# The low halves of the HGRN and mLSTM weights, formed by VectorE alone

## The chip, the cores and the metric

One core of one Trainium2 chip. The metric is the device time of one execution in microseconds, taken as the median of several runs. The profile is that of one further execution.

## The reference, cut to what matters

One layer over 256 latent tokens with 256 context tokens ahead of them, width 1024, all in fp32. A combined projection `w_in` feeds two recurrent branches: HGRN2 with 8 heads, and an mLSTM with 4 heads. Their outputs are merged and go through a mixture of 32 experts.

```python
p_lat = jnp.split(h_lat @ w_in + b_in, SEG_OFFSETS[:-1], axis=-1)
p_ctx = jnp.split(h_ctx @ w_in + b_in, SEG_OFFSETS[:-1], axis=-1)
...
o_ctx, hs_f, hs_b = hgrn_core(p_ctx[0], p_ctx[1], p_ctx[2], p_ctx[3], lb, s0, s0)
o_lat, _, _ = hgrn_core(p_lat[0], p_lat[1], p_lat[2], p_lat[3], lb, hs_f, hs_b)
...
for e in range(N_EXPERTS):
    a = jax.nn.silu(tok @ w_gate[e]) * (tok @ w_up[e])
    out = out + combine[:, e:e + 1] * (a @ w_down[e])
```

## The kernel before, in words

**How a product with `w_in` is made.** The fp32 weights arrive in tiles `raw` of 128x2048 (1 MB). Each is split into a high half `whi`, which ScalarE rounds in two copies of 1024 columns, and a low half `wlo = raw - whi`. The activations are split in the same way (`hhi`, `hlo`), and a product is three series of matmuls on TensorE: high by high (L362, or L371 where the weights are the stationary operand), low activations by high weights (L363, L372), and high activations by low weights (L365, L374). A split's `wlo` is thus the last thing that its product needs.

**Who forms the low half.** `load_split_` (L223 to L236) gives columns 0 to 256 x (8 - kp) to VectorE and the rest to GpSimd. The constant `KH` is the kp of the HGRN branch, `MKP` that of the mLSTM heads, `GKP` that of the merge and of the output projection. With `KH, MKP, GKP = 2, 3, 2` VectorE has 1536 columns of an HGRN split and GpSimd 512; in an mLSTM split it is 1280 and 768.

**Stages.** About 22 us of start, then the adaLN modulation and first products up to 57 us. Then HGRN works in four pairs of heads (p = 0 to 3) up to about 306 us, five splits a pair, of which the first two of p = 0 are formed elsewhere: 18 splits of `load_split`. The four mLSTM heads follow, three splits each (12 splits), up to about 440 us. The merge of the branches has 20 splits (`GKP`). From 565 us on the experts' weights stream in, and the matmuls of the experts follow them.

**What sets the order.** The code is written for a scheduler that puts the instructions of all engines into in-order queues, by priorities (`PRIO`) and by its own estimates of durations. An engine works down its queue; an instruction that waits holds up all behind it. The work of the next pair or head is thus laced into that of the present one. Buffers bound the lacing: `raw` has 3 tiles and one more in a ring, `whi` and `wlo` 2 each, and PSUM has 3 banks `mm`, 2 `lv`, 2 `oo` and a single bank `tp` for transposes.

**Names that come up below.** An HGRN pair has gates on VectorE and GpSimd (`fl`, `fc` at L635, L637; `kl`, `kc` at L641, L642), transposes of `kd` through `tp` (L698), state matmuls (L704), and eight levels, each with small matmuls (L720, L744) and updates of `xa` and `kl` on VectorE (L759, L762). `xa` is first formed by GpSimd (L708). The gates of the mLSTM are prepared in between as small operations (`gz`, `r`, `rr`, L543 to L579). A column of the modulation is summed up on VectorE (`adac`, L315 and L317), transposed through the same bank `tp` (L324) and read out of it by a reduction on VectorE (L326). An mLSTM head convolves `q` and `k` on VectorE (`cz`, L864 and L866), transposes `k` through `tp` (L897), sums its state (L907), copies it out on VectorE (`cs`, L908) and reads it in L949.

Of the kernel before, what the change touches and what calls it, by code (L numbers as in the profile page):

```python
# [19 lines left out]
NQ = NE // 4  # L20
CAP = 32
RZ, RP, RA, RB, RC = 2, 2, 2, 5, 7
KH, MKP, GKP = 2, 3, 2
NWARM, NW0 = 2, (7, 2, 1)
MLG = 2
ADP = (1, 3)
# [1458 lines left out]
```

## Time and profile before

| what | value |
|---|---|
| median of 3 runs | 1005.48 us (1004.79 to 1009.0) |
| the profiled execution's own time | 1005.86 us |
| its span in the trace | 1003.8 us |
| TensorE matmuls, busy | 862.8 us |
| VectorE, busy | 477.0 us |
| ScalarE, busy | 277.9 us |
| GpSimd, busy | 191.2 us, 130 instructions |
| moved by DMA | 290.50 MB, 289 GB/s on the mean |

The shares are means over stages with different limits. From 57 to 565 us TensorE is nearly always busy while the DMA engines are at a third to nine tenths; from 565 us on the DMA engines are busy throughout and TensorE is not. The profiled execution lies 0.4 us above the median, and 2.1 us of its time lie outside the span.

### The profile page before, as it was taken

Reading aid. Unit: us, or ns where it says so; the run is one execution under the profiler, and the core shown is the slowest. Engines: PE = TensorE matmul, PEld = TensorE weight load, DVE = VectorE, ACT = ScalarE, POOL = GpSimd, SP = SyncE. Lnnn points to the kernel's source line nnn. Section 1 sums busy time; section 2 is a strip of 40 time slices with the busy share of each in tenths; the row PEclk is TensorE's granted clock in tenths of the full one; section 3 lists DMA queues with packets and bytes.
Section 4 is the critical chain, followed back from the end, with each engine's and each line's share of the span. In section 5 each row is a group of like instructions: output and inputs, shape, how many; then the busy total and the mean of one; then the engine's idle time right before and its main releaser. Section 6 shows DMA issues by size and latency. Waiting matters only on the chain.

```text
span 1003.8 us, 15963 instructions
## 1 busy us (share of the span) xinstructions
PE 862.8 (86%) x6687; PEld 591.7 (59%) x6687; DVE 477.0 (48%) x908; ACT 277.9 (28%) x430; POOL 191.2 (19%) x130
## 2 busy tenths in 40 slices
PE   7999999979998999999999999767686767777865
PEld 3588897968978898999999644213031220313312
DVE  3678779798667988874465422102020110202002
ACT  4564433643323553444443210000000000000101
POOL 0053441535503232124434000000000000000000
PEclk9999999989999999999999999879778776978978
DMA  9733345255243445248887999999999999999996
GB/s 372 287 130 133 126 137 193 98 191 187 96 164 114 165 147 167 83 159 321 300 332 277 373 423 426 426 425 423 428 424 427 425 424 388 419 426 424 426 424 265
DMA packets 45610, 290.50 MB, mean 289 GB/s; under 512 B 5216, under 2 KB 10336, under 8 KB 11104
## 3 DMA queue, kind: packets, MB, share of 16 engines
q1 hardware_dynamic: 45248, 288.94, 72.8%
q8 instruction: 53, 0.87, 0.3%
q10 hardware_dynamic: 288, 0.52, 0.1%
q14 instruction: 21, 0.17, 0.0%
HBM read 288.23 MB, written 1.21 MB: 288 GB/s over the span
## 4 chain that ended last, share of the span: by engine, by line
issue 45%; PE 41%; DVE 8%; ACT 3%; DMA 2%; POOL 1%; SPq 0%; POOLq 0%; DVEq 0%; ACTq 0%
PE mm L365 5%; PE mm L362 5%; PE mm L363 5%; PE mm L374 2%; PE mm L372 2%; PE mm L371 2%; PE mm L1102 2%; PE mm L1099 2%; PE mm L1100 2%; DMA raw<-in_win_dram 2%; PE mm L412 2%; DVE wlo L158 1%; PE mm L1240 1%; ACT whi L155 1%; PE oo L952 1%
## 5 line engine op out<-in xcount | busy, mean ns | idle before, releaser
L158 POOL TENSOR_TENSOR wlo<-raw,whi 128x512 fp32r<-128x512 f32 (+1 forms) x50 | 112.7, 2254 | 197.4 <-ACT whi L155 166.3
L155 ACT ACTIVATE whi<-raw 128x1024 fp32r<-128x1024 f32 x104 | 105.6, 1052 | 104.6 <-POOL wlo L158 26.3
L362 PE MATMUL mm<-hhi,whi 128*128 128x256 f32 (+1 forms) x448 | 132.2, 322 | 0.0
L363 PE MATMUL mm<-hlo,whi 128*128 128x256 f32 (+1 forms) x448 | 130.1, 317 | 0.0
L158 DVE TENSOR_TENSOR wlo<-raw,whi 128x1536 fp32r<-128x1536 f32 (+2 forms) x54 | 108.1, 2004 | 34.1 <-ACT whi L155 30.6
L158 DVE TENSOR_TENSOR a<-a,mm 128x512 f32<-128x512 f32 x8 | 5.5, 688 | 233.5 <-PE mm L1240 233.5
L362 PEld LDWEIGHTS mm<-hhi,whi 128*128 128x128 f32 x448 | 85.5, 191 | 4.8
L363 PEld LDWEIGHTS mm<-hlo,whi 128*128 128x128 f32 x448 | 85.5, 191 | 4.4
L1378 POOL TENSOR_TENSOR rsn<-rsn,con 128x2 f32<-128x2 f32 x1 | 0.7, 698 | 434.7 <-DVE rsn L158 434.7
L365 PE MATMUL mm<-hhi,wlo 128*128 128x256 f32 (+1 forms) x448 | 80.7, 319 | 0.9 <-POOL wlo L158 0.9
L365 PEld LDWEIGHTS mm<-hhi,wlo 128*128 128x128 f32 x448 | 65.8, 191 | 5.8 <-POOL wlo L158 1.1
L1214 DVE SCALAR_TENSOR_TENSOR x<-oo,mod,x 128x256 f32<-128x256 f32 x56 | 24.4, 480 | 88.3 <-PE oo L1273 88.3
L1240 PE MATMUL mm<-ub,xg 128*32 128x512 f32 x304 | 50.3, 734 | 17.3 <-DMA ub<-in_eu_dram 9.9
L371 PE MATMUL mm<-whi,hhi 128*128 128x256 f32 x256 | 63.1, 284 | 0.0
L372 PE MATMUL mm<-whi,hlo 128*128 128x256 f32 x256 | 62.9, 283 | 0.0
L371 PEld LDWEIGHTS mm<-whi,hhi 128*128 128x128 f32 x256 | 49.1, 192 | 0.2
L372 PEld LDWEIGHTS mm<-whi,hlo 128*128 128x128 f32 x256 | 49.1, 192 | 0.1
L155 ACT ACTIVATE aT<-tp 128x512 f32<-128x512 f32 x8 | 4.8, 597 | 148.1 <-PE tp L1252 148.1
L1273 PE MATMUL oo<-owT,y 128*128 128x256 f32 x112 | 35.3, 470 | 8.6 <-ACT y L155 8.6
L1240 PEld LDWEIGHTS mm<-ub,xg 128*32 128x32 f32 x304 | 8.3, 120 | 56.4 <-DMA ub<-in_eu_dram 24.8
L1264 PE MATMUL lv<-uc,aT 128*32 128x512 f32 x280 | 36.1, 604 | 5.6 <-DMA uc<-in_ed_dram 5.6
L1273 PEld LDWEIGHTS oo<-owT,y 128*128 128x128 f32 x112 | 24.6, 230 | 27.4 <-ACT y L155 21.0
(391 smaller groups left out, 1588.3 us busy)
## 6 DMA issues: line engine op xcount, KB each, us to landing
uc<-in_ed_dram SPq DMA_DIRECT2D x35, 1024.0 KB, 19.8
raw<-in_win_dram SPq DMA_DIRECT2D x32, 1024.0 KB, 5.0
raw<-in_wm_dram SPq DMA_DIRECT2D x20, 1024.0 KB, 5.0
ub<-in_eg_dram SPq DMA_DIRECT2D x20, 1024.0 KB, 19.4
ub<-in_eu_dram SPq DMA_DIRECT2D x18, 1024.0 KB, 19.5
raw<-in_wada_dram SPq DMA_DIRECT2D x16, 1024.0 KB, 4.9
uB<-in_eu_dram SPq DMA_DIRECT2D x14, 1024.0 KB, 19.6
uc<-in_eu_dram SPq DMA_DIRECT2D x14, 1024.0 KB, 19.7
```

The source lines that it names most:

```text
L155: return S.activation(o, i, f, **kw)
L158: return (e or V).tensor_tensor(o, a, b, op=op)
L362: T.matmul(o, a, hhi[:, k, c0:c0 + n], start=(k == 0), stop=False)
L363: T.matmul(o, a, hlo[:, k, c0:c0 + n], start=False, stop=False)
L365: last = T.matmul(o, lo[:, k, 128 * m:128 * m + 128], hhi[:, k, c0:c0 + n], start=False, stop=(k == 7))
L371: T.matmul(o, hhi[:, k, c0:c0 + 128], hi[:, k, :], start=(k == 0), stop=False)
L372: T.matmul(o, hlo[:, k, c0:c0 + 128], hi[:, k, :], start=False, stop=False)
L374: T.matmul(o, hhi[:, k, c0:c0 + 128], lo[:, k, :], start=False, stop=(k == 7))
L1214: V.scalar_tensor_tensor(o, r[:, n * a:n * a + n], mod[:, 0, 40 + c + a:41 + c + a], o, op0=ALU.mult, op1=ALU.add)
L1240: last = T.matmul(r[32 * i:32 * i + 32, :], xg[:, k, 32 * i:32 * i + 32], W[k][:, 512 * i:512 * i + 512], start=(k == 0), stop=(k == 7), t ...
L1264: T.matmul(r[32 * i:32 * i + 32, 0:n], aT[:, k, 32 * i:32 * i + 32], w[k][:, o:o + n], start=(k == 0), stop=(k == 3), tile_position=(0, 32 ...
L1273: last = T.matmul(r[:, 256 * a_:256 * a_ + 256], y[:, 128 * (c + a_):128 * (c + a_) + 128], owT, start=True, stop=True)
```

## The change

`KH` and `MKP` become 0. With kp = 0 the loop in `load_split_` gives VectorE one operation of 2048 columns, and GpSimd's slice is empty and is left out. So 18 operations of VectorE grow from 1536 to 2048 columns, 12 grow from 1280 to 2048, and 30 operations of GpSimd (18 of 512 columns, 12 of 768) are gone. The 20 splits of the merge stay as they are.

```diff
-KH, MKP, GKP = 2, 3, 2
+KH, MKP, GKP = 0, 0, 2
```

The scheduler makes other queues from it. The order of the TensorE queue differs between about 252 and 1460 of its 2584 rows, which is from the second HGRN pair to the third mLSTM head; the merge and the experts keep theirs. Three places matter below.

The first is TensorE's queue where the HGRN pair p = 2 hands over to p = 3. L365 is the end of a product of p = 2, L698 the transpose of `kd` of p = 2, the 512-wide L362 and L363 are the first product of p = 3, and L720 the levels of p = 2. Before:

```order
L365 MATMUL mm<-hhi,wlo 128x256 x7
L698 MATMUL tp<-con,kd 128x128 x4
L365 MATMUL mm<-hhi,wlo 128x256
L720 MATMUL lv<-q,t_2210 32x32
L720 MATMUL lv<-xa,yk 32x32 x16
L720 MATMUL lv<-q,t_2210 32x32 x15
L362 MATMUL mm<-hhi,whi 128x512
L704 MATMUL oo<-v,kt 128x128 x4
```

Now, from the row in which that L698 stands:

```order
L698 MATMUL tp<-con,kd 128x128 x4
L362 MATMUL mm<-hhi,whi 128x512
L363 MATMUL mm<-hlo,whi 128x512
L720 MATMUL lv<-xa,yk 32x32 x16
L704 MATMUL oo<-v,kt 128x128 x4
L698 MATMUL tp<-con,kd 128x128 x2
L744 MATMUL lv<-xa,kl 32x32 x16
L698 MATMUL tp<-con,kd 128x128 x2
L704 MATMUL oo<-v,kt 128x128 x4
L324 MATMUL tp<-con,adac 128x128 x4
L365 MATMUL mm<-hhi,wlo 128x512 x3
```

The L365 is now at row 724, with all 8, and L698 follows 37 rows later: ahead of it come 30 of the 512-wide matmuls of p = 3 and four groups of L720.

The second is VectorE's queue at the same place, up to the reduction L326 that reads the bank `tp` out. Before (the wide `wlo` stands 8 rows ahead of these):

```order
L158 TENSOR_TENSOR v<-mm,br 128x512
L315 TENSOR_SCALAR adac<-raw,sgc 128x512
L575 TENSOR_SCALAR gz<-gz 40x128
L317 SCALAR_TENSOR_TENSOR adac<-raw,sgc,adac 128x512
L543 SCALAR_TENSOR_TENSOR gz<-gz,con 40x255
L317 SCALAR_TENSOR_TENSOR adac<-raw,sgc,adac 128x512
L158 TENSOR_TENSOR gz<-gz 40x256
L317 SCALAR_TENSOR_TENSOR adac<-raw,sgc,adac 128x512
L579 TENSOR_SCALAR gz<-gz,mle 40x256
L317 SCALAR_TENSOR_TENSOR adac<-raw,sgc,adac 128x512
L326 TENSOR_REDUCE mod<-tp 128x4
L317 SCALAR_TENSOR_TENSOR adac<-raw,sgc,adac 128x512
```

Now (the `wlo` of 2048 columns stands 23 rows ahead of these, and the `adac` operations directly behind it):

```order
L158 TENSOR_TENSOR v<-mm,br 128x512
L738 COPY_PREDICATED adg<-lm,lv 128x128
L759 TENSOR_TENSOR xa<-xa,tot_2242 128x128x2x2
L762 TENSOR_TENSOR kl<-kl,tot_2290 128x32x2x8
L158 TENSOR_TENSOR gz<-gz 40x256
L738 COPY_PREDICATED adg<-lm,lv 128x128
L759 TENSOR_TENSOR xa<-xa,tot_2266 128x64x2x4
L579 TENSOR_SCALAR gz<-gz,mle 40x256
L762 TENSOR_TENSOR kl<-kl,tot_2314 128x16x2x16
L326 TENSOR_REDUCE mod<-tp 128x4
L738 COPY_PREDICATED adg<-lm,lv 128x128
L759 TENSOR_TENSOR xa<-xa,tot_2290 128x32x2x8
```

The reduction has moved from 18 to 32 rows behind its `wlo`: the whole `adac` series (seven L317) and three updates each of `xa` and `kl` are now in front of it.

The third is TensorE's queue at the first mLSTM head, where `k` is transposed (L897) and the state read (L949). The 512-wide product is head 1's, as the 256-wide one in `lv` is. Before:

```order
L362 MATMUL mm<-hhi,whi 128x512
L897 MATMUL tp<-con,k 128x128 x2
L912 MATMUL lv<-q,k 128x256 x2
L907 MATMUL oo<-v,wk 128x257 x4
L362 MATMUL lv<-hhi,whi 128x256
L363 MATMUL lv<-hlo,whi 128x256
L362 MATMUL lv<-hhi,whi 128x256
L363 MATMUL lv<-hlo,whi 128x256
L362 MATMUL lv<-hhi,whi 128x256
L949 MATMUL oo<-cs,qi 128x257
```

Now:

```order
L365 MATMUL mm<-hhi,wlo 128x512 x2
L897 MATMUL tp<-con,k 128x128 x2
L912 MATMUL lv<-q,k 128x256 x2
L362 MATMUL lv<-hhi,whi 128x256
L363 MATMUL lv<-hlo,whi 128x256
L907 MATMUL oo<-v,wk 128x257 x4
L362 MATMUL lv<-hhi,whi 128x256
```

Ten more rows of head 1's product stand in front of L897, and the first L949 has gone from 8 rows behind it to 20.

## Rows read from the trace of the kernel before

**Rows 1.** Windows by stage: us, engines' busy time (instructions), PEclk, DMA share, GB/s.

```profile
187.00:255.00 68.00, 60.81 (x603) 53.12 (x602) 60.57 (x104) 34.90 (x49) 30.91 (x16) 0.95 0.45 160
...
306.00:340.00 34.00, 30.41 (x210) 27.93 (x209) 30.14 (x66) 13.71 (x24) 7.90 (x7) 1.00 0.51 159
...
640.00:1003.80 363.80, 259.54 (x1614) 85.10 (x1612) 49.00 (x121) 22.45 (x46) 0.70 (x1) 0.80 0.98 411
```

**Rows 2.** TensorE's waits: total, times, longest; windows 57:125, 125:187, 187:255, 275:306, 306:340, 374:410.

```profile
PE lv L720 <- DVE xa L759: 1.0, 1, 1.0
...
PE lv L720 <- DVE xa L759: 1.3, 1, 1.3
...
PE tp L698 <- DVE mod L326: 6.0, 1, 6.0
PE mm L365 <- POOL wlo L158: 0.9, 1, 0.9
...
PE lv L720 <- DVE xa L759: 1.6, 2, 1.3
...
PE tp L897 <- DVE k L158: 2.1, 1, 2.1
PE oo L949 <- DVE cs L908: 1.4, 1, 1.4
...
PE oo L949 <- DVE cs L908: 1.3, 1, 1.3
```

**Rows 3.** Windows of seven and eight us at TensorE's longest wait; columns as in Rows 1.

```profile
210.00:217.00 7.00, 1.01 (x7) 0.83 (x6) 6.99 (x17) 2.85 (x6) 0.00 (x0) 0.71 0.48 153
217.00:225.00 8.00, 8.00 (x155) 6.33 (x154) 7.92 (x12) 5.12 (x8) 2.57 (x1) 0.82 1.00 364
```

**Rows 4.** Timeline, VectorE, then GpSimd, ahead of that wait's end.

```profile
201.50 1.72 DVE L158 TENSOR_TENSOR wlo<-raw,whi 128x1536 fp32r<-128x1536 f32 x1
203.15 4.08 DVE L158 TENSOR_TENSOR r<-gz 8x256 f32<-8x256 f32 x2
...
215.44 0.67 DVE L326 TENSOR_REDUCE mod<-tp 128x4 f32<-128x512 f32 x1
...
200.95 4.59 POOL L158 TENSOR_TENSOR xa<-fl,q 128x1024 f32<-128x1024 f32 x1 [7.56 <-DVE q L656]
...
207.90 1.29 POOL L158 TENSOR_TENSOR wlo<-raw,whi 128x512 fp32r<-128x512 f32 x1
```

**Rows 5.** Timeline, GpSimd, then VectorE, of one HGRN split.

```profile
173.18 2.87 POOL L158 TENSOR_TENSOR wlo<-raw,whi 128x512 fp32r<-128x512 f32 x1 [8.11 <-ACT t L155]
...
173.14 1.76 DVE L158 TENSOR_TENSOR wlo<-raw,whi 128x1536 fp32r<-128x1536 f32 x1 [0.69 <-ACT t L155]
174.82 1.38 DVE L635 TENSOR_SCALAR fl<-sg,oml,lbt 128x256 f32<-128x256 f32 x1
```

**Rows 6.** Timeline, VectorE: a split of 1024 columns, and one `fl` operation by itself.

```profile
37.46 1.22 DVE L158 TENSOR_TENSOR wlo<-raw,whi 128x1024 fp32r<-128x1024 f32 x1
...
162.22 0.41 DVE L635 TENSOR_SCALAR fl<-sg,oml,lbt 128x256 f32<-128x256 f32 x1 [0.42 <-ACT sg L155]
```

**Rows 7.** Groups by form: count | busy us, mean ns | idle before, releasers.

```profile
L158 POOL TENSOR_TENSOR wlo<-raw,whi 128x512 fp32r<-128x512 f32 x38 | 86.2, 2270 | 157.3 <-ACT whi L155 126.2 <-PE mm L365 11.6 <-issue 8.4
...
L158 DVE TENSOR_TENSOR wlo<-raw,whi 128x1536 fp32r<-128x1536 f32 x38 | 77.4, 2038 | 32.9 <-ACT whi L155 29.4 <-PE mm L365 2.7 <-ACT t L155 0.7
...
L317 DVE SCALAR_TENSOR_TENSOR adac<-raw,sgc,adac 128x512 f32<-128x512 f32 x49 | 40.4, 824 | 0.5
...
L759 DVE TENSOR_TENSOR xa<-xa,tot 128x512 f32<-128x512 f32 x28 | 19.3, 691 | 3.9 <-PE lv L744 1.9 <-PE lv L755 1.3 <-PE lv L720 0.4
```

**Rows 8.** Timeline, TensorE: two neighbouring matmuls of a 512-wide product.

```profile
220.58 0.39 PE L362 MATMUL mm<-hhi,whi 128*128 128x512 f32 x1
220.81 0.40 PE L363 MATMUL mm<-hlo,whi 128*128 128x512 f32 x1
```

**Rows 9.** Timeline, VectorE, at the last HGRN pair and the first mLSTM head.

```profile
280.29 2.58 DVE L759 TENSOR_TENSOR xa<-xa,fl 128x512 f32<-128x512 f32 x1 [0.59 <-PE lv L720]
...
311.89 1.98 DVE L864 TENSOR_SCALAR cz<-qin,pk 128x256 f32<-128x256 f32 x1
...
326.96 3.13 DVE L158 TENSOR_TENSOR wlo<-raw,whi 128x1280 fp32r<-128x1280 f32 x1
```

## The prediction

> **What bounds the kernel now.** I read the windows by stage first, then TensorE's waits in the stages that matter, then the timeline around each wait. From 640 us to the end the DMA engines are at 0.98 of their time and move 411 GB/s while TensorE works 259.5 of 363.8 us: the experts' weights are the bound there, and the change doesn't touch them [rows 1]. Before the merge it is TensorE: 60.8 of 68 us from 187 to 255, 30.4 of 34 from 306 to 340. VectorE is close behind, 60.6 and 30.1 us of the same stretches. So in the stages that the change touches, time can be won only in TensorE's gaps, and few gaps hold nearly all of it: 6.0 us and 0.9 in the stretch from 187 to 255, 1.6 at the last HGRN pair, 2.1 + 1.4 at the first mLSTM head, 1.3 at the third, and 1.0 and 1.3 in the two stretches from 57 to 187 [rows 2]. That is 15.6 us. All but the 0.9, which waits for GpSimd, end with an operation of VectorE, and that one may be late for its own work, for GpSimd's, or for its place in the queue. A gap closed ahead of the experts should reach the end nearly whole, since the experts' buffers come free at TensorE's pace; the bound of it is a rival below.
>
> **What the two engines do to each other.** A VectorE split of 1536 columns takes 1.76 us even beside GpSimd [rows 5], one of 1024 takes 1.22 [rows 6], so 512 columns are worth 0.54 and an operation of 2048 should take about 2.30 us (an estimate). GpSimd's 512 columns take 1.29 us by themselves [rows 4], but 2.87 when started beside VectorE, and the VectorE operation behind the split, an `fl` that takes 0.41 alone [rows 6], then takes 1.38 [rows 5]. The engines take turns. The whole low half was ready 2.91 us after VectorE's start (173.14 to 176.05); formed by VectorE alone it would be ready after 2.30. So the price of 0.54 us on VectorE per HGRN split (0.80 for the 768 columns of an mLSTM split, by the same slope) meets 0.97 us that the next operation gets back, and `wlo` comes no later. By the means (1536 columns 2.04 us, GpSimd's 512 columns 2.27) the turns cost VectorE's splits themselves some 0.28 us each on top [rows 7]. Over 18 and 12 splits the price is 18 x 0.54 + 12 x 0.80 = 19.3 us on VectorE if nothing comes back.
>
> [...]
>
> **The sum, place by place.**
>
> *HGRN pair p = 2 to p = 3.* TensorE stood 6.0 us, up to 216.3, in front of the L698 for the single bank `tp`, which the reduction L326 at 215.44 had to read out [rows 2, 4]. VectorE was busy through it (6.99 of 7.0), and lost time in it: two `r` operations took 4.08 us beside GpSimd's `xa` of 4.59 and its 512-column `wlo` [rows 3, 4]. Two small operations of this kind take about 0.4 us each (an estimate by the `fl` of that size), so 3.2 us went there. The change takes away the `wlo` share of this, about 1.0, but not `xa`'s 2.2. In the new queue the reduction stands behind more: three further `adac` operations of at most 0.82 us, three updates of `xa` at 0.69 and three of `kl`, taken as equal, so 3 x (0.82 + 2 x 0.69) = 6.6, 0.54 for the wider split [rows 7], and about 0.7 for small copies (an estimate). That puts its end at 215.44 + 0.67 + 6.6 + 0.54 + 0.7 - 1.0 = 223.0 at worst; with what earlier splits give back (0.43 net each, three since 187 us) 221.6; with `xa`'s stall gone too 219.4. TensorE in the meantime has other work: 30 matmuls at 0.23 us [rows 8] and four groups of small ones at about half a microsecond, together 8.9 us that used to lie behind the wait. So it reaches L698 at about 219.2 and waits 0 to 4 us there, and the gain is 216.3 + 8.9 minus the time at which L698 starts: 2.2 at the worst, 3.6 in the middle, 5.8 at best. The granted clock was 0.71 and 0.82 of full speed after the long gap [rows 3]; at full speed the eight busy us of the second stretch are 8 x 0.18 = 1.4 us shorter. I take 3.6 + 1.4 = **-5.0**; bounds -2.2 and -8.3 (6.0, 0.9 and 1.4).
>
> *First mLSTM head.* The 2.1 us wait is for `k`, the 1.4 for `cs` [rows 2]. Ahead of `k` VectorE pays 2 x 0.80 and gets back 1.98 less some 0.4 at L864 and about 1.1 at a later step of the convolution, so `k` is no later. TensorE now has ten more matmul rows, at 0.23 us 2.3 us, in front of L897, and 12 more in front of L949. The split in front of `cs`, 3.13 us beside GpSimd, should take 2.30 [rows 9]. Both waits should go: **-3.3** of 3.5; bound 0, if `k` slips as much as TensorE's cover grows.
>
> *Last HGRN pair.* The first `xa` update took 2.58 us at 280.29, beside GpSimd's share of a split [rows 9]; it does more than the 0.69 of the later ones [rows 7], about 1.1 (an estimate). TensorE waited 1.6 us for it and the next [rows 2]. The queue keeps its order. **-1.2**; bounds 0 and -1.6.
>
> *Third mLSTM head.* 1.3 us for `cs` [rows 2], with the same 0.80 of price ahead of it and the same kind of return. I take half: **-0.6**; bounds +0.8 and -1.3.
>
> Elsewhere TensorE hardly waits, but for the 1.0 and 1.3 us before 187, for `xa`, where the queue's order changes too. There I count nothing (bounds -2.3, and the new wait of rival 1): the splits run ahead of their matmuls, and the cover is VectorE's own spare time, 3.9 us of 34 in the first head [rows 1], against 2.4 for its three splits. The `raw` loads, which wait for old splits, come by VectorE's end and not GpSimd's, so no later. Sum: -10.1, from the profiled 1005.86 to 995.8; the median lies 0.4 below that execution, hence **995.4 us**.
>
> **Rivals.**
>
> 1. *VectorE's queue absorbs it (same).* At 187 to 255 VectorE is busy 60.6 of 68 us [rows 1]; if the levels behind the handover wait for it anyway, that place gives 2 instead of 5, the third head nothing, and the changed order leaves a wait of a microsecond or two in the first pairs. Then -2.2 - 2.0 - 0.7 + 1.5 = -3.4, about 1002. For it speaks the reduction's new place behind 14 more operations; against it that GpSimd's work comes out of the way in the same stretch.
> 2. *The experts' DMA absorbs it (same).* If the weights' stream from 565 us on were paced by something other than freed buffers, a front 10 us earlier would end in a longer wait for weights: 1004 to 1006. The DMA share before the experts, 0.45 and 0.51 [rows 1], says that the queue then waits for buffers, so I give it little.
> 3. *The split's own price decides (slower).* If the stalls beside GpSimd mostly have another cause, VectorE pays 0.54 us on five splits from 187 to 255, where it has no slack, = 2.7, and two splits, 1.6 us, in front of `k` in the two heads where TensorE waits, = 3.2: +5.9, 1011.4. It decides from where less than 0.54 of the 0.97 us per HGRN split comes back. The 1.38 against 0.41 of the `fl` speaks against it [rows 5, 6]. [...]
>
> **How the numbers follow.** 0.5% is 5 us, about what a measurement of this kernel can tell from no change. Forecast 0.66, with its own range 988 to 1000.4 (all bounds below, -8.3 - 3.5 - 1.6 - 1.3 - 2.3 = -17.0; half of the sum). Rivals 1 and 2 together 0.20, rival 3 0.14. Faster 0.66, same 0.20, slower 0.14. The range goes from 987.5 to 1005: below it 0.04, above it rival 3 and a little of rival 2.
>
> **What would show it.** In the changed trace: VectorE's 2048-column splits near 2.3 us; `fl` at 0.41 behind them; no TensorE wait of 6 us at L698, and a granted clock of 1.00 from 210 to 225; no waits at L897 and L949 of the first head; the merge some 10 us earlier, and the start of the experts as well. I am wrong if a new wait of some us for VectorE stands at L698, at a level's L720 or at a matmul that reads `wlo` (L365, L374), or if the merge comes earlier and the end does not.

## The result and the profile after

| kernel | median, us | runs | ratio to before on the same chip, 95% interval |
|---|---|---|---|
| before | 1006.04 | 4, 1004.79 to 1009.0 | |
| changed | 995.16 | 4, 991.58 to 995.92 | 0.9875 [0.9855, 0.9895] |

The forecast was 995.4 us and faster. The ratio is worth 0.0125 x 1006 = 12.6 us, the medians 10.9. The profiled execution of the changed kernel took 991.58 us with a span of 989.6, which is the lowest of its four, so the two profiles are 14.2 us apart. The traces show where that is won. First the page, part 1, of the kernel after:

```profile
PE 859.9 (87%) x6687; PEld 595.1 (60%) x6687; DVE 465.3 (47%) x908; ACT 280.3 (28%) x432; POOL 126.0 (13%) x100
```

VectorE is busy 465.3 us against 477.0, although its splits grew. GpSimd lost 65 us. The merge's first matmuls on the high half of the weights (L1099) date the end of the part that the change touches. One line's count, shortest, median and longest duration in ns, and its first and last start in us, of the kernel before and then after:

```profile
L1099 PE MATMUL mm<-yah,whi x64: 278/283/362, 484.4 to 506.3; 128*128 128x256 f32 x64
```

```profile
L1099 PE MATMUL mm<-yah,whi x64: 278/283/363, 471.0 to 493.0; 128*128 128x256 f32 x64
```

The merge starts 13.4 us earlier (484.4 to 471.0), and the span ends 14.2 earlier: what was won in front reached the end whole. Two windows of the kernel before that stand in no row so far, with the columns of [rows 1]:

```profile
57.00:125.00 68.00, 66.50 (x637) 56.38 (x636) 51.01 (x88) 32.56 (x49) 31.92 (x23) 1.00 0.37 128
125.00:187.00 62.00, 60.32 (x609) 53.01 (x609) 50.57 (x86) 23.64 (x36) 23.23 (x16) 1.00 0.45 156
```

These two and the windows of [rows 1] and [rows 3], in the kernel after:

```profile
57.00:125.00 68.00, 67.86 (x651) 58.18 (x650) 51.54 (x89) 32.48 (x49) 20.56 (x17) 1.00 0.37 126
125.00:187.00 62.00, 61.63 (x620) 54.18 (x620) 51.11 (x88) 25.00 (x37) 16.83 (x12) 1.00 0.46 158
187.00:255.00 68.00, 63.81 (x639) 56.33 (x638) 62.23 (x111) 40.74 (x56) 18.97 (x12) 1.00 0.50 173
...
306.00:340.00 34.00, 33.96 (x234) 31.61 (x233) 30.92 (x73) 16.51 (x26) 3.97 (x6) 1.00 0.50 174
...
210.00:217.00 7.00, 5.76 (x113) 4.02 (x114) 6.95 (x19) 5.47 (x10) 0.00 (x0) 1.00 0.58 191
217.00:225.00 8.00, 7.25 (x118) 5.70 (x117) 7.22 (x12) 5.91 (x8) 0.00 (x0) 1.00 0.65 216
```

TensorE's gap from 306 to 340 us is gone (33.96 of 34 busy, 30.41 before), that from 187 to 255 is down from 7.2 to 4.2, those from 57 to 187 are down from 3.2 to 0.5 in sum, and the granted clock stays at 1.00 from 210 to 225, where it was 0.71 and 0.82 [rows 3]. It falls at another place instead, behind a 0.8 us wait for `rsn` (L348) at the last HGRN pair. The window behind that wait in the kernel after, then at the same matmuls in the kernel before (PEclk is third from the end):

```profile
297.00:301.00 4.00, 4.00 (x24) 4.00 (x23) 1.56 (x3) 0.82 (x1) 0.17 (x3) 0.57 0.05 16
```

```profile
306.00:310.00 4.00, 4.00 (x36) 4.00 (x35) 2.09 (x4) 2.13 (x3) 0.00 (x0) 1.00 0.09 25
```

The same 20 matmuls (12 of L362 and L363, 8 of L365) take 3.97 us there where they took 2.48, so 1.5 us are lost. The kernel before has the same 0.8 us wait and no such fall, and so has the changed kernel when it runs again in experiment 4: the fall does not come with the change every time.

What is left from 187 to 255 us are new, shorter waits (TensorE's waits: total, times, longest):

```profile
PE oo L771 <- DVE xa L759: 2.0, 1, 2.0
PE mm L362 <- DVE v L158: 0.8, 1, 0.8
PE oo L704 <- ACT kt L155: 0.7, 1, 0.7
PE lv L720 <- ACT adg L155: 0.7, 1, 0.7
```

The timeline of VectorE and then GpSimd around the handover, against [rows 4]:

```profile
196.07 2.93 DVE L543 TENSOR_TENSOR_SCAN gz<-gz,con 40x128 f32<-40x128 f32 x2
...
199.15 2.29 DVE L158 TENSOR_TENSOR wlo<-raw,whi 128x2048 fp32r<-128x2048 f32 x1 [0.15 <-ACT whi L155]
...
201.76 0.41 DVE L158 TENSOR_TENSOR r<-gz 8x256 f32<-8x256 f32 x1
...
202.86 0.42 DVE L158 TENSOR_TENSOR r<-gz 8x256 f32<-8x256 f32 x1
...
216.19 0.68 DVE L326 TENSOR_REDUCE mod<-tp 128x4 f32<-128x512 f32 x1
...
196.26 2.46 POOL L158 TENSOR_TENSOR xa<-fl,q 128x1024 f32<-128x1024 f32 x1 [8.86 <-DVE q L656]
```

And the two scans of L543 in the kernel before:

```profile
200.85 0.72 DVE L543 TENSOR_TENSOR_SCAN gz<-gz,con 40x128 f32<-40x128 f32 x2
```

The two `r` take 0.41 and 0.42 us where they took 4.08 together, and `xa` takes 2.46 and not 4.59. The stall beside `xa` has not vanished: it falls on the two scans, 2.93 us instead of 0.72. They stand ahead of the split, which still waited 0.15 us for its `whi` after them, so the stall made nothing behind it late. The reduction starts at 216.19, 0.75 us later than before with 14 more operations in front of it, and ends at 216.87; TensorE comes to L698 at 217.37, half a microsecond later. The splits and the `fl` behind them, as groups by form (count, busy us, mean ns, idle before), after, and the `fl` of the kernel before:

```profile
L158 DVE TENSOR_TENSOR wlo<-raw,whi 128x2048 fp32r<-128x2048 f32 x30 | 69.8, 2327 | 10.7 <-ACT whi L155 8.5 <-PE mm L365 2.1
...
L635 DVE TENSOR_SCALAR fl<-sg,oml,lbt 128x256 f32<-128x256 f32 x16 | 7.7, 480 | 9.5 <-ACT sg L155 9.4
```

```profile
L635 DVE TENSOR_SCALAR fl<-sg,oml,lbt 128x256 f32<-128x256 f32 x16 | 11.9, 746 | 8.1 <-ACT sg L155 8.1
```

The 30 splits take 69.8 us. At the means of the kernel before, 2.04 us for 1536 columns [rows 7] and 2.16 for 1280, they were 18 x 2.04 + 12 x 2.16 = 62.6, so VectorE's splits cost 7.2 more and everything else on VectorE 18.9 less. The `fl` fell from 0.75 to 0.48 us on the mean.

### The profile page after: what moved, and what is told of

It reads as the page before. It is cut to its first block, busy times and chain, and to the rows that moved or that the text cites. A ratio compares the mean times of both kernels' runs of the same rounds, so it can differ in the third digit from the quotient of the medians.

```text
span 989.6 us, 15883 instructions
## 1 busy us (share of the span) xinstructions
PE 859.9 (87%) x6687; PEld 595.1 (60%) x6687; DVE 465.3 (47%) x908; ACT 280.3 (28%) x432; POOL 126.0 (13%) x100
## 4 chain that ended last, share of the span: by engine, by line
issue 48%; PE 43%; ACT 3%; DVE 3%; DMA 2%; POOL 1%; SPq 0%; POOLq 0%; DVEq 0%; ACTq 0%
PE mm L362 6%; PE mm L363 5%; PE mm L365 5%; PE mm L374 2%; PE mm L372 2%; PE mm L371 2%; PE mm L1102 2%; PE mm L1099 2%; PE mm L1100 2%; PE mm L412 2%; DMA raw<-in_win_dram 2%; PE mm L1240 1%; PE oo L952 1%; ACT whi L155 1%; PE oo L907 1%
## 5 line engine op out<-in xcount | busy, mean ns | idle before, releaser
L362 PE MATMUL mm<-hhi,whi 128*128 128x256 f32 (+1 forms) x448 | 131.7, 321 | 0.8 <-DVE v L158 0.8
L158 DVE TENSOR_TENSOR wlo<-raw,whi 128x2048 fp32r<-128x2048 f32 (+2 forms) x54 | 116.4, 2156 | 30.2 <-ACT whi L155 27.9
L363 PE MATMUL mm<-hlo,whi 128*128 128x256 f32 (+1 forms) x448 | 130.0, 317 | 0.0
L362 PEld LDWEIGHTS mm<-hhi,whi 128*128 128x128 f32 x448 | 85.4, 191 | 6.1 <-DVE v L158 1.2
L363 PEld LDWEIGHTS mm<-hlo,whi 128*128 128x128 f32 x448 | 85.4, 191 | 4.5
L365 PE MATMUL mm<-hhi,wlo 128*128 128x256 f32 (+1 forms) x448 | 80.4, 318 | 0.0
L365 PEld LDWEIGHTS mm<-hhi,wlo 128*128 128x128 f32 x448 | 65.3, 191 | 4.5
L1240 PE MATMUL mm<-ub,xg 128*32 128x512 f32 x304 | 52.3, 761 | 16.6 <-DMA ub<-in_eg_dram 8.6
L158 POOL TENSOR_TENSOR wlo<-raw,whi 128x512 fp32r<-128x512 f32 x20 | 45.0, 2248 | 84.6 <-ACT whi L155 81.7
L641 POOL TENSOR_SCALAR kl<-sg,oml 128x256 f32<-128x256 f32 x16 | 26.4, 1648 | 117.8 <-ACT sg L155 117.8
```

Source lines behind the costliest of these rows:

```text
L158: return (e or V).tensor_tensor(o, a, b, op=op)
L362: T.matmul(o, a, hhi[:, k, c0:c0 + n], start=(k == 0), stop=False)
L363: T.matmul(o, a, hlo[:, k, c0:c0 + n], start=False, stop=False)
L365: last = T.matmul(o, lo[:, k, 128 * m:128 * m + 128], hhi[:, k, c0:c0 + n], start=False, stop=(k == 7))
L641: G.tensor_scalar(kl[:, d, 256 * m:256 * m + 256], sn[:, 0:256], oml[:, d, h:h + 1], None, op0=ALU.mult)
L1240: last = T.matmul(r[32 * i:32 * i + 32, :], xg[:, k, 32 * i:32 * i + 32], W[k][:, 512 * i:512 * i + 512], start=(k == 0), stop=(k == 7), t ...
```

## The experiments

**1. Each half alone.** Theory: TensorE's gaps close one by one, and what each part of the change closes adds up. Rival: VectorE's relief is one pool, and half of the change does little.

```diff
-KH, MKP, GKP = 0, 0, 2
+KH, MKP, GKP = 0, 3, 2      # one run
+KH, MKP, GKP = 2, 0, 2      # the other
```

> KH = 0 with MKP = 3 as before: only the HGRN splits are formed by VectorE alone, and TensorE's queue is that of the change up to the mLSTM and that of before from there on. Theory (the gain is TensorE's gaps closed place by place, and adds up): the gaps from 84 to 255 us and the clock behind the long one, about 2.7 + 3.0 + 1.1 us, so 6 to 7.5 us faster than before, near 999. Rival (the gain hangs on both parts together, since VectorE's relief is one pool): less than 4 us here.

> MKP = 0 with KH = 2 as before. Theory: the 6.0 us gap at L698 stays; the last HGRN pair, which is laced with the first head's splits, and the heads' waits for k and cs go, about 1.6 + 3.5 + 1.2 us, so 5 to 6.5 us faster than before, near 1000. The two gains add up to the change's 11 to 13. Rival (one pool): less than 3 us here, and the two together clearly less than the change.

Measured: HGRN alone 1000.32 us, ratio 0.9918 [0.9901, 0.9936]; mLSTM alone 1001.27, 0.9925 [0.9909, 0.9941]. That is 8.3 and 7.6 us, each about 1 us above its expected range, and 15.9 together, against 12.6 of the change in the first comparison and 13.8 in experiment 4. The sum is 2 to 3 us too large, about as much as the intervals allow, and each half does much alone, which the one pool of the rival does not. TensorE's waits of the HGRN kernel from 306 to 340 us, then of the mLSTM kernel from 187 to 255:

```profile
PE tp L897 <- DVE k L158: 2.1, 1, 2.1
PE oo L949 <- DVE cs L908: 1.4, 1, 1.4
```

```profile
PE tp L698 <- DVE mod L326: 6.0, 1, 6.0
PE mm L365 <- POOL wlo L158: 0.9, 1, 0.9
```

In these windows each kernel keeps the waits of the half that it left as it was [rows 2].

**2. GpSimd's work put back without a use.** Nobody reads the result; the used-up `raw` tile is overwritten.

```diff
...
+        if kp == 0:
+            n = 768 if pr == "ls_m" else 512
+            tt(r[:, 0:n], r[:, 0:n], hi[:, 0:n].bitcast(F32), ALU.subtract, G)
```

> The changed kernel, and behind each of the 30 VectorE splits a subtraction of 512 (HGRN) or 768 (mLSTM) columns on GpSimd that is written into the used-up raw tile and read by nobody. TensorE's and VectorE's queues are almost those of the change. Theory (the turns on SBUF that GpSimd took from VectorE are what was removed): GpSimd's operations last 1.3 and 1.8 us and hold up VectorE as before, with VectorE's wider splits on top, so nearly all of the gain is lost: 1002 to 1010. Rival (the new order of the queues is what gains, not GpSimd's absence): 995 to 998.

Measured: 1009.62 us, ratio 1.0012 [1.0001, 1.0023]. The whole gain is gone, though TensorE's queue differs from the changed kernel's in 36 lines of some 2600 only. The page, part 1; the useless operations; and TensorE's waits from 57 to 570 us:

```profile
PE 860.6 (85%) x6687; PEld 593.1 (59%) x6687; DVE 488.8 (48%) x908; ACT 281.0 (28%) x432; POOL 176.4 (17%) x130
```

```profile
L158 POOL TENSOR_TENSOR raw<-raw,whi 128x768 f32<-128x768 f32 x12 | 27.2, 2269 | 57.2 <-DVE wlo L158 52.3 <-DVE mod L158 5.0
L158 POOL TENSOR_TENSOR raw<-raw,whi 128x512 f32<-128x512 f32 x18 | 26.7, 1486 | 88.0 <-DVE wlo L158 41.1 <-issue 28.7 <-ACT ain L155 18.3
```

```profile
PE lv L723 <- DVE xa L762: 5.3, 7, 2.0
PE tp L900 <- DVE k L158: 2.4, 1, 2.4
PE oo L774 <- DVE mod L158: 2.0, 1, 2.0
```

(The lines are 3 further down than in the changed kernel.) VectorE, which was given nothing to do, is busy 488.8 us, 23.5 more. TensorE waits for it at seven places for `xa`, and for `k` again.

**3. The order of the queues at the handover.** The first product of p = 3 is held behind the first L698 of p = 2, as before.

```diff
...
-                    last = mm_ch(r, w, m, 0, 512)
+                    with tc.issue_after(kdt[0].ins) if p == 3 and d == 0 else nullcontext():
+                        last = mm_ch(r, w, m, 0, 512)
...
+                if d == 0:
+                    kdt[0] = tr         # the last transpose of L698
```

> The changed kernel, but the first product of pair p = 3 is put behind the first L698 of p = 2 on TensorE, which is the order of before at this place. Theory (at this place the order is half of the gain, since VectorE's reduction is no earlier than before: 216.2 against 215.4 us): TensorE waits again some 7 us around L698, of which up to 3.5 come back later, because the waits of 0.7 to 2.0 us behind it find work: 3 to 7 us slower than the change, 998 to 1002. Rival (GpSimd's absence alone gains, whatever the order): at most 1 us slower than the change, 995 to 996.

Measured: 997.64 us, ratio 0.9896 [0.988, 0.9913]. Against the change's 0.9875 and 0.9863 that is 2 to 3 us, between the rival's 1 and the theory's 3 to 7, and the intervals overlap; the trace is clearer. TensorE's longest waits from 57 to 570 us, and the window of [rows 3], in this kernel:

```profile
PE lv L724 <- ACT adg L155: 4.1, 1, 4.1
PE lv L724 <- DVE xa L763: 2.5, 2, 1.4
...
PE tp L700 <- DVE mod L326: 0.5, 1, 0.5
```

```profile
210.00:217.00 7.00, 1.97 (x96) 1.60 (x96) 6.95 (x19) 6.86 (x12) 0.00 (x0) 0.56 0.48 167
```

TensorE is busy for 1.97 of 7 us and the granted clock falls to 0.56. It idles in front of the levels (L724 here, L720 before), not at the transposes as I had expected: the levels come first in its queue, and the longest of these waits, 4.1 us, ends with ScalarE's copy `adg`. So the laced-in product of p = 3 does cover work of VectorE and ScalarE there.

**4. Is it reading, or being busy? And what is VectorE's time worth?** Three kernels and the change itself once more, on one chip. In the first, GpSimd's useless subtraction is a memset of about the same length; in the second the useless subtraction runs on VectorE; in the third the merge's splits are given to VectorE too. The first two edits are shown against the kernel of experiment 2, the third against the change.

```diff
-            tt(r[:, 0:n], r[:, 0:n], hi[:, 0:n].bitcast(F32), ALU.subtract, G)
+            G.memset(r[:, 0:n], 0.0)      # n = 1540 or 1100
...
-            tt(r[:, 0:n], r[:, 0:n], hi[:, 0:n].bitcast(F32), ALU.subtract, G)
+            tt(r[:, 0:n], r[:, 0:n], hi[:, 0:n].bitcast(F32), ALU.subtract)
...
-KH, MKP, GKP = 0, 0, 2
+KH, MKP, GKP = 0, 0, 0
```

> The changed kernel once more, on the chip of the next three, so that they can be set against it. All theories: 11 to 13 us faster than before, a ratio of 0.987 to 0.989.

> As the run with the useless subtraction, but GpSimd's 30 operations are memsets of the used-up raw tile (1100 or 1540 columns, so about 1.3 and 1.8 us by the 0.61 of a 520-column memset): GpSimd is as long busy and its kl, kc and xa queue behind it, but it reads nothing. Theory (VectorE is held up where both read SBUF): nearly none of the gain is lost, within 3 us of the change. Rival (GpSimd's own queue, kl, kc and xa coming late behind the splits, was the loss): as the subtraction, some 14 us above the change.

> The changed kernel with a further, useless subtraction of 512 (HGRN) or 768 (mLSTM) columns on VectorE behind each of the 30 splits: 18 x 0.54 + 12 x 0.80 = 19.3 us more of VectorE's time at the least, no GpSimd. It prices VectorE's time by itself, the third rival of the prediction. Theory (the same time that GpSimd's turns took, taken in another way, costs nearly the same per us): 5 to 12 us slower than the change. Rival (VectorE has slack, and GpSimd does harm in some other way than by VectorE's time): at most 2 us slower.

> GKP = 0 too: the 20 splits of the merge on VectorE alone. Theory (only TensorE's gaps are worth anything): TensorE is busy for 91 of 91 us from 440 to 531 in both kernels, so nothing changes beyond 1 us either way, and at most the 0.8 and 0.6 us waits for VectorE at the end of the merge move a little. Rival (GpSimd's absence frees VectorE and with it the weights' buffers earlier): 2 us or more faster than the change.

| kernel | median, us | ratio, 95% interval |
|---|---|---|
| change again | 992.61 | 0.9863 [0.984, 0.9885] |
| memset on GpSimd | 991.63 | 0.9843 [0.9822, 0.9865] |
| subtraction on VectorE | 997.41 | 0.99 [0.9882, 0.9917] |
| merge too | 992.42 (one of five executions took 1085.17) | 0.9851 [0.9829, 0.9873] |

The memsets cost nothing that can be measured. They are a little shorter than I had reckoned; as groups by form:

```profile
L238 POOL MEMSET raw<- 128x1100 f32 x18 | 18.5, 1030 | 86.5 <-DVE wlo L158 61.6 <-issue 24.9
...
L238 POOL MEMSET raw<- 128x1540 f32 x12 | 17.0, 1421 | 57.6 <-DVE wlo L158 40.1 <-issue 17.5
```

So GpSimd being occupied, with `kl`, `kc` and `xa` behind it, is not the loss; 35.5 us of operations that only write did no harm, where 53.9 us that read two tiles cost 14 to 15. Nor is it that the used-up `raw` comes free later: by the DMA queue's waits from 57 to 440 us, 27 loads wait for GpSimd's memset and 28 for its subtraction. The merge's splits don't matter, as expected: TensorE has hardly a gap there (90.62 of 91 us busy from 440 to 531 in the changed kernel). The subtraction on VectorE was a miss, 4.8 us by the medians and 3.7 by the ratios where 5 to 12 was expected, and it left a riddle: VectorE is busy 487.0 us in it, as long as beside GpSimd's subtractions (488.8), for a third of the loss. Its page, part 1:

```profile
PE 865.2 (87%) x6687; PEld 595.3 (60%) x6687; DVE 487.0 (49%) x938; ACT 277.5 (28%) x430; POOL 128.6 (13%) x100
```

**5. Split and order taken apart.** The scheduler had planned the queues around VectorE's useless work (hundreds of lines of difference on TensorE's against those 36), but cannot plan around GpSimd's turns. So the next three kernels fix the order: each row of the TensorE and VectorE queues is tied to the row ahead of it in the other kernel's queue (issue order alone, no wait). The edit is shortened here.

```diff
+    def keep_order():
+        ...
+            for a, b in zip(o, o[1:]):      # o: the wanted order of the engine's instructions
+                tc.add_manual_dep(mine[b], mine[a].name, NoSync, reason="order")
```

> The kernel before, KH = 2 and MKP = 3, with the TensorE and VectorE queues put row by row into the order of the changed kernel. GpSimd takes its turns as before. Theory (the turns are the loss, and the order matters little): the gain is lost, 1003 to 1009. Rival (the order is the gain): 993 to 998. Half and half: 999 to 1002.

> The changed kernel, KH = MKP = 0, with the TensorE and VectorE queues put row by row into the order of before. Theory: without GpSimd's turns the reduction L326 comes some 5 us earlier than in the kernel before (3.2 and 0.9 us of stalls and an earlier start, against 0.5 of price), so that the 6.0 us wait at L698 shrinks to about 1 in the old order too, and so do the waits for k and cs: 993 to 998, within 4 us of the change. Rival (the order is the gain): 1004 to 1008. Half and half: 999 to 1002.

> The run with the useless VectorE subtractions, with all other rows of the TensorE and VectorE queues in the order of the changed kernel, so that the queues were not planned around the extra 22 us. Theory (GpSimd's turns cost VectorE about as much, 23.5 us, and cost 16 us in the end because the order was not planned around them): 1000 to 1008. Rival (VectorE's own time is cheap wherever it stands, and a turn of GpSimd's does more harm than its length on VectorE): within 2 us of the same run in its own order, which was 997.4.

| ratio, 95% interval | order of before | order of the change |
|---|---|---|
| GpSimd has a share | 1 | 1.0029 [1.0018, 1.004], 1010.58 us |
| VectorE alone | 0.9928 [0.9913, 0.9944], 1001.04 us | 0.9875 and 0.9863 |
| VectorE alone, useless work on VectorE | | 0.9999 [0.9988, 1.001], 1008.09 us |

The new order by itself gains nothing; beside GpSimd's turns it is even 3 us slower, 1.6 above the range expected for a lost gain. (No kernel was tied to its own order, so what the tie costs by itself is not shown.) The split by itself gains 7 us in the old order, half of the change and less than the 993 to 998 that I had expected. TensorE's waits in that kernel from 57 to 570 us:

```profile
PE tp L701 <- DVE mod L329: 4.3, 1, 4.3
PE tp L900 <- DVE k L160: 1.6, 1, 1.6
```

The reduction does come 5.1 us earlier (at 210.39, from the timeline), as expected, but TensorE is also 3.4 us earlier at L698, so that 4.3 of the 6.0 us stay. Below, the reduction and that transpose in the timeline:

```profile
210.39 0.67 DVE L329 TENSOR_REDUCE mod<-tp 128x4 f32<-128x512 f32 x1
```

```profile
211.21 1.09 PE L701 MATMUL tp<-con,kd 128*128 128x128 f32 x4 [4.28 <-DVE mod L329]
```

And the riddle is solved: with the queues kept as they were, VectorE's useless work costs the whole gain, as GpSimd's does. 486.1 - 465.3 = 20.8 us more of VectorE cost about 0.0130 x 1008 = 13 us (0.6 us for each us), while those 21.7 that the scheduler knew of cost 3.7 to 4.8 (0.2 for each us). TensorE's longest waits in this kernel:

```profile
PE oo L778 <- DVE xa L766: 3.1, 1, 3.1
PE tp L904 <- DVE k L160: 2.6, 1, 2.6
PE mm L369 <- DVE v L160: 2.5, 1, 2.5
```

**6. One step further.** GpSimd's other frequent operations that read SBUF in these stages, the gates `kl` and `kc` (L641, L642), go to ScalarE, on top of `merge_too`.

```diff
-                    G.tensor_scalar(kl[:, d, 256 * m:256 * m + 256], sn[:, 0:256], oml[:, d, h:h + 1], None, op0=ALU.mult)
-                    G.tensor_scalar(kc[:, d, m, :], sn[:, 256:512], oml[:, d, h:h + 1], None, op0=ALU.mult)
+                    act(kl[:, d, 256 * m:256 * m + 256], sn[:, 0:256], AF.Copy, scale=oml[:, d, h:h + 1])
+                    act(kc[:, d, m, :], sn[:, 256:512], AF.Copy, scale=oml[:, d, h:h + 1])
```

> KH, MKP and GKP all 0, and kl and kc (L641, L642), 32 operations of GpSimd of 1.3 to 1.6 us, on ScalarE instead, so that GpSimd has only xa and small work left in the HGRN. Theory (each GpSimd operation that reads SBUF costs VectorE time where VectorE is nearly saturated): TensorE's gaps of 4.2 us from 187 to 255 shrink, 1 to 3 us faster than the change, 989.5 to 992. Rival (ScalarE, busy 40.7 of 68 us there, becomes late with the copies that TensorE's levels wait for): 1 to 4 us slower than the change.

Measured: 987.82 us (986.33 to 987.96), ratio 0.9799 [0.9786, 0.9811], faster than both kernels: 6.5 us below the change (0.9863) by the ratios and 5.2 below `merge_too` (0.9851), which it differs from by these gates alone; 1 to 3 were expected. Its window from 187 to 255 us, and TensorE's longest waits for VectorE and for ScalarE from 57 to 570:

```profile
187.00:255.00 68.00, 66.14 (x659) 58.74 (x658) 63.42 (x115) 43.96 (x63) 4.00 (x3) 1.00 0.49 169
```

```profile
PE mm L362 <- DVE v L158: 1.0, 1, 1.0
...
PE oo L704 <- ACT kt L155: 0.7, 1, 0.7
```

TensorE is busy 66.1 of 68 us there, and the 2.0 us wait for the last `xa` has gone. ScalarE, at 44.0, is late for TensorE only where it was late in the change, 0.7 us for `kt`. The waits are about half of the gain, though. In the two profiles the merge (L1099) starts 4.8 us apart, at 466.4 here and at 471.2 in `merge_too`. TensorE's waits from 57 to 570 us went from 7.6 to 5.1 us, which is 2.5 and in the range expected. Another 1.5 us are the fall of the granted clock at 297 us, which `merge_too`'s profile has as the change's, and this one has not. Whether the gates had a part in that isn't shown.

## Why the prediction was right, step by step

- *The price and the turns.* Right. A split of 2048 columns takes 2.29 us undisturbed (2.30 forecast), `fl` fell to 0.48 on the mean (0.41 forecast, and reached only when the gates leave GpSimd too, in experiment 6), and the turns are the cause: putting GpSimd's reads back takes the whole gain (1009.62 us), a memset of GpSimd takes none (991.63), and each half of the change removes its own waits. In those two runs VectorE is busy 23.5 and 5.4 us more than in the changed kernel, beside 53.9 us of GpSimd's subtractions and 35.5 us of its memsets.
- *The handover.* -5.0 was forecast, 1.4 of it for the clock. The gap shrank by 3.0 us (7.2 to 4.2). The clock gave back about 1.3 here (an estimate: the operations from the first L698 to the last L704 took 4.0 us in the kernel before, 216.26 to 220.26, and about 2.7 at the durations that they have in the changed kernel). So it is about 4.3, but by errors that cancel in part. I had `xa`'s stall of 2.2 us hold up the reduction; it fell on the scans ahead of the split and cost nothing. I had the two `r` meet the GpSimd split of 207.90 [rows 4]; the one that they met began at 205.49 and took 1.46 us, and that of 207.90 held up two copies `rr` behind them (1.58 us, 0.28 each now), a further 1.0 us that I left out. So the reduction ended at 216.87 and not at 221.6, and TensorE did not wait at L698 at all, but at four other places, 4.2 us in sum, for VectorE's `xa` and `v` and for ScalarE's `kt` and `adg`. For this place the first rival had such waits at the levels behind the handover; its 1.5 us of new waits in the first pairs did not come.
- *The mLSTM heads.* -3.3 and -0.6; the first head's 3.5 went whole, and in the changed kernel no wait is left from 306 to 440 us, so the third head gave 1.3. By experiment 5 the wait for `k` needs both: with the split alone 1.6 of the 2.1 us stay.
- *The last HGRN pair.* -1.2; its 1.6 went. The 1.5 us that the fall of the clock at 297 us took in this profile stood in no term.
- *Elsewhere.* 0 was forecast, and this is the term that was mis-sized: 2.7 us came from 57 to 187 us (gaps of 3.2 us before, 0.5 after), where the 1.0 and 1.3 us waits for `xa` went too. I had put them into the bounds alone.
- *The sum.* The terms measured give 4.3 + 3.5 + 1.3 + 1.6 + 2.7 - 1.5 = 11.9 of the 13.4 us at the merge. The other 1.5 are not put down to a place; most of them is TensorE's busy time from 22 us to the merge (440.6 before, 439.5 after), and not the clock, whose two effects nearly cancel there. That 995.4 met 995.16 is in part luck: the profiles are 14.2 us apart and the ratios say 12.6 and 13.8, where 10.1 was forecast, and the term put at nothing is most of that.
- *The end.* Right: 13.4 us at the merge, 14.2 at the end. The second rival, an end that absorbs it, is out.
- *The third rival.* VectorE's own time does have a price, 0.6 us for each us where the queues are not planned around it; that a split gives back more than it takes is why the sign came out as forecast. 19.3 us of price stand against 11.7 less on VectorE in the whole, so 31.0 us were returned. Taking the work back gained 12.6 us; experiment 6 moved GpSimd's gates to ScalarE and gained too, 5.2 us below `merge_too`.

What the forecast treated as two causes side by side, the turns and the order, are not two terms of a sum. The order gains nothing beside GpSimd's turns and 5 to 7 us without them.

## What to carry to other kernels

Before a busy VectorE is relieved by GpSimd, compare the operation behind the shared one with the same operation elsewhere in the trace. Here the `fl` behind the split took 1.38 us against 0.41, 0.97 us more for the 0.54 that GpSimd took over [rows 5, 6], so nothing was saved; and the stall falls on whatever stands next in the queue, as on the two `r` before (4.08 us) and on the two scans after (2.93). A scheduler that doesn't know these turns plans queues around durations that do not hold. Here taking the turns out gained twice: 7 us in the old order, and 5 to 7 more in the order that was planned for the new split. For two gates ScalarE was the better helper than GpSimd (0.51 and 0.50 us each against 1.65 and 1.29); look for such a helper only in the stages where the matmul engine has gaps: the merge's splits, where TensorE was busy 90.62 of 91 us, moved the median by 0.2 us (992.61 to 992.42).

## What the runs showed that I had not expected

- The same 21 us of added VectorE time cost 4 to 5 us when the queues were planned with it and 13 when they were not.
- GpSimd's operations that only write (30 memsets, 35.5 us in all) made the kernel no slower, though VectorE was busy for 77 to 94% of the windows from 57 to 255 us. VectorE's own busy time rose by 5.4 us (465.3 to 470.7), mostly in operations with one input tile: four `cz` from 0.54 to 1.02 us on the mean, sixteen `fl` from 0.48 to 0.58, eight `rt` from 0.35 to 0.49. The 30 splits, with two, rose by 0.4 us in all.
- The granted clock fell to half of full speed behind 297 us in the changed kernel's profile (0.50 from 298 to 300) and in `merge_too`'s, and not in the second profile of the changed kernel and in that of experiment 6 (1.00 from 255 to 306 in both), behind the same 0.8 us wait for `rsn`; the 32 matmuls L362 of that form (`lv`, 128x256) took 335 and 337 ns on the mean in the first two and 311 in the others: 1.5 us by which two profiles differ without any edit.
- GpSimd's gates took 1.36 and 1.39 us on the mean in the kernel before and 1.65 and 1.29 in the changed one (groups by form, 16 each); ScalarE does the same work in 0.51 and 0.50, below, and the `fl` are down to 0.41 us.

```profile
L155 ACT ACTIVATE kl<-sg,oml 128x256 f32<-128x256 f32 x16 | 8.2, 510 | 0.4
...
L155 ACT ACTIVATE kc<-sg,oml 128x256 f32<-128x256 f32 x16 | 8.0, 497 | 0.0
```
